# Packing the state-space parameters and the first input on the host, a shifted tap load, Y in column strips, and new planner costs

## The chip, the cores and the metric

The kernel runs on one core of a Trainium2 chip. The time is device time in microseconds, one launch of the whole program; lower is better. The core has TensorE (PE), VectorE (DVE), ScalarE (ACT), GpSimd (POOL) and SyncE (SP), which here issues all DMA loads and stores of the program. Every engine takes its own instructions strictly in the order of its queue.

## The reference

A sequence of 256 tokens of width 1024 goes through two blocks in float32. The first has four layers; each is a mixer (differential attention, stick-breaking attention, sliding-window attention with a sink, differential attention again) and a SwiGLU feed-forward, with an RMS norm before and after each. The second block has dilated attention on one half of the width and, on the other half (512 channels in 32 groups of 16), a diagonal complex state-space model (S5) of 64 states per group, and then a gated projection of an extra input p. Cut to the state-space part, which the change concerns most:

```python
dt = exp(log_dt)[:, None]
a = exp(lam_re * dt) * (cos(lam_im * dt) + i sin(lam_im * dt))
bb = (a - 1) / lam * (b_re + i b_im)
bu = einsum('bsgc,gnc->bsgn', u, bb)
x[s] = a * x[s-1] + bu[s]
y = einsum('bsgn,gcn->bsgc', x_re, c_re) - einsum('bsgn,gcn->bsgc', x_im, c_im) + d_skip * u
yg = gelu(y)
out = yg * sigmoid(yg @ w_glu + b_glu)
```

The rest of the work is mostly dense products of the 256 tokens with weights.

## The kernel before, in words

**Dense products.** Tokens are in two halves b of 128 (NB = 2). To reach float32 accuracy each operand is split into a high and a low part (fp32r), and each product runs three passes. A weight chunk of 1 MB (128 x 2048 elements) is loaded into one of three buffers `raw`; ScalarE makes the high part and VectorE the low part (`w`, 11 buffers, two splits for a chunk on each engine); on TensorE the activations are stationary, and 512 columns of the weights move per pass into a PSUM tile `acc`. The activations are `hnT` (normed input, transposed), `hT` (hidden of the feed-forward) and `oT` (attention output). `prenorm` (L717) turns x with TensorE transposes `tr`, multiplies by the transposed gains gT and splits.

**State space.** Time is cut into 32 blocks k of 8 steps t. `ssm_prep_tasks` (L1196) computes, during the first layers, what depends on the parameters alone: `params` (L1214) loads them with 39 DMAs into `pp` and `pt` and clears the taps, `coef` (L1255) forms the discretised coefficients on GpSimd, ScalarE and VectorE and turns C with TensorE (`cT`), `powers` (L1303) the powers of a (tiles `q`), and `part_e`, eight times (L1322), wide GpSimd products of 128 x 256, which TensorE transposes (`eT`) and multiplies (`ke`) into the taps, the response within 15 steps. `part_g` (L1356) makes G, which leads from states to outputs. E, G and taps are stored in DRAM (`scrE`, `scrG`, `taps`). These tasks are spread over the first layers' steps.

In the second block `ssm_in` (L1387) makes U, the inputs of each block of time; `ssm_scan` (L1406) forms S = E U with 64 small matmuls, copies it from PSUM to X, and VectorE and GpSimd run the scan over the 32 blocks; `ssm_y` (L1455) adds taps times U and G times X in two PSUM tiles Y: 32 tap products with 128-column taps stationary (loaded in two rounds of eight DMAs) and 32 moving columns, and 32 products with G stationary (loaded in four rounds of four DMAs), on a copy X2 of X that has the real part over the imaginary one. Y is copied out, written to DRAM (`scr_y`), read back transposed, and goes through the Gelu. Dense products of attention's q, k, v and gates are recorded around these steps.

**What sets the order.** The code only records the engine calls (`record`, L209). `_Program` gives each a cost in nanoseconds (`passes` L170 for TensorE, `cost` L185 for the others and for DMAs), with edges for data and for buffers that are used again (`ring_edges` L261) and for the first loads in a list by hand (`head_edges` L284). `schedule` (L426) then runs a list scheduler forward and backward from several random starts, keeps the order whose modelled end is the earliest, and `issue` (L456) issues that order; all instructions have line L464 in the profile. So a changed cost or a dropped operation can move any instruction on any engine. The costs of a dense pass and of a GpSimd operation before are

```python
load, stream, k = cols / 1.2, n * (1.0 if n >= 256 else 4.0) / 2.4, 1
return 150 + (1.66 if op == ALU.mult else 2.1) * n
```

**Start.** `setup` (L544) loads the gains and x, turns the gains with one transpose, starts the first weights, and sets the order of the first loads in `nc.head`; `warm` (L572) runs eight matmuls while they come.

## Time and profile before

| what | us |
|---|---|
| runs of the kernel before, three | 1449.31, 1451.95, 1452.11 |
| median | 1451.95 |
| span of the profiled execution | 1446.5 |
| its own time, beside the span | not listed apart; the runs shown lie 2.8 to 5.6 over the span |
| TensorE busy | 1399.7 |
| VectorE, ScalarE, GpSimd busy | 900.2, 774.7, 163.4 |

The profile is of one execution, and its times count from the start of its span. A busy TensorE is not necessarily one at its peak: the clock that it was granted (PEclk, 1.00 is full) is listed by stretch. The views used are the page's table of busy times, its table of DMA issues, the chain of waits (start, length, engine and tile, number of instructions), the timeline of an engine (start, length, engine, line, operation, tile written and tiles read, shape, count, and in brackets the idle time before it with what ended it), and the table of stretches.

### The profile page before, as it was taken

Reading aid. Unit: us, or ns where it says so; the run is one execution under the profiler, and the core shown is the slowest. Engines: PE = TensorE matmul, PEld = TensorE weight load, DVE = VectorE, ACT = ScalarE, POOL = GpSimd, SP = SyncE. Lnnn points to the kernel's source line nnn. Section 1 sums busy time; section 2 is a strip of 40 time slices with the busy share of each in tenths; the row PEclk is TensorE's granted clock in tenths of the full one; section 3 lists DMA queues with packets and bytes.
Section 4 is the critical chain, followed back from the end, with each engine's and each line's share of the span. In section 5 each row is a group of like instructions: output and inputs, shape, how many; then the busy total and the mean of one; then the engine's idle time right before and its main releaser. Section 6 shows DMA issues by size and latency. Waiting matters only on the chain.

```text
span 1446.5 us, 18484 instructions
## 1 busy us (share of the span) xinstructions
PE 1399.7 (97%) x7093; PEld 1157.0 (80%) x7093; DVE 900.2 (62%) x1311; ACT 774.7 (54%) x1261; POOL 163.4 (11%) x258
## 2 busy tenths in 40 slices
PE   8999969699999999999999999999999999998998
PEld 6788847578788788888878888887888888887887
DVE  7967526556855755557856456588766555676274
ACT  6656525334776754445656454456665444562572
POOL 0001039961200000000000000010010000010000
PEclk9999989899999999999999999999999999997999
DMA  8644527554634455555334555554445555467641
GB/s 265 204 146 153 182 27 258 164 191 160 212 116 146 143 192 178 197 178 180 128 116 141 194 180 196 182 187 147 151 154 204 175 190 185 156 218 149 197 147 54
DMA packets 153360, 243.95 MB, mean 169 GB/s; under 512 B 23016, under 2 KB 45880, under 8 KB 153272
## 3 DMA queue, kind: packets, MB, share of 16 engines
q1 hardware_dynamic: 153272, 242.77, 51.7%
q8 instruction: 56, 0.92, 0.3%
q14 instruction: 32, 0.26, 0.1%
HBM read 235.97 MB, written 6.78 MB: 168 GB/s over the span
## 4 chain that ended last, share of the span: by engine, by line
PE 86%; POOL 6%; SPq 3%; DVE 2%; DMA 2%; issue 1%; ACT 1%; DVEq 0%; POOLq 0%
PE acc L464 73%; POOL pt L464 4%; PE tr L464 4%; SPq L464 3%; PE sS L464 2%; PE sc L464 2%; PE Y L464 1%; PE z L464 1%; PE oS L464 1%; DMA scrM<-taps 1%; POOL pp L464 1%; PE o L464 1%; DVE w L464 1%; POOL q L464 1%; PE asT L464 0%
## 5 line engine op out<-in xcount | busy, mean ns | idle before, releaser
L464 PE MATMUL acc<-w,hnT 128*128 128x512 f32 (+1 forms) x3744 | 849.7, 381 | 3.0 <-ACT hnT L464 1.0
L464 PEld LDWEIGHTS acc<-w,hnT 128*128 128x128 f32 x3744 | 664.2, 190 | 133.4 <-issue 4.8
L464 DVE TENSOR_TENSOR w<-raw,w 128x1024 fp32r<-128x1024 f32 (+1 forms) x431 | 519.3, 1220 | 195.6 <-ACT w L464 185.9
L464 ACT ACTIVATE w<-raw 128x1024 fp32r<-128x1024 f32 (+1 forms) x431 | 442.1, 1041 | 194.2 <-PE acc L464 151.8
L464 PE MATMUL acc<-w,hT 128*128 128x512 f32 x1056 | 256.6, 398 | 13.2 <-ACT hT L464 13.0
L464 PEld LDWEIGHTS acc<-w,hT 128*128 128x128 f32 x1056 | 198.6, 191 | 54.9 <-ACT hT L464 13.4
L464 PE MATMUL acc<-w,oT 128*128 128x512 f32 x480 | 119.2, 397 | 0.0
L464 PEld LDWEIGHTS acc<-w,oT 128*128 128x128 f32 x480 | 87.9, 188 | 19.8 <-issue 2.3
L464 POOL TENSOR_TENSOR po_r<-po_v,neghalf 128x1 f32<-128x1 f32 x16 | 13.8, 862 | 751.5 <-DVE po_v L464 751.4
L464 ACT ACTIVATE sg<-acc,pn_r 128x512 f32<-128x512 f32 (+1 forms) x48 | 31.2, 650 | 81.2 <-PE acc L464 77.3
L464 DVE SCALAR_TENSOR_TENSOR sg<-acc,pn_r,sg 128x512 f32<-128x512 f32 (+1 forms) x48 | 33.8, 704 | 50.2 <-PE acc L464 40.4
L464 ACT ACTIVATE hT<-tr 128x512 fp32r<-128x512 f32 (+1 forms) x48 | 26.7, 556 | 71.1 <-PE tr L464 71.0
L464 POOL TENSOR_TENSOR pt<-pp 128x256 f32<-128x256 f32 x64 | 50.6, 808 | 42.9 <-PE ke L464 41.0
L464 DVE TENSOR_TENSOR hT<-tr,hT 128x512 fp32r<-128x512 f32 (+1 forms) x48 | 30.9, 644 | 30.6 <-ACT hT L464 30.5
L464 DVE TENSOR_TENSOR facc<-acc,facc 128x512 f32<-128x512 f32 x32 | 21.9, 687 | 33.7 <-PE acc L464 33.7
L464 POOL TENSOR_TENSOR pn_r<-pn_v,neghalf 128x1 f32<-128x1 f32 x20 | 16.2, 810 | 213.0 <-DVE pn_v L464 201.0
L464 ACT ACTIVATE ad_e<-sc,ad_nm 128x128 f32<-128x128 f32 (+1 forms) x64 | 26.1, 422 | 24.2 <-DVE ad_nm L464 20.6
L464 ACT ACTIVATE hnT<-gx 128x512 fp32r<-128x512 f32 x40 | 25.1, 627 | 20.0 <-DVE gx L464 19.9
L464 POOL TENSOR_TENSOR pt<-pt 128x256 f32<-128x256 f32 x32 | 35.5, 1108 | 2.0
L464 ACT ACTIVATE sqj<-x 128x512 f32<-128x512 f32 x40 | 24.9, 625 | 18.6 <-DVE x L464 13.8
L464 DVE TENSOR_REDUCE as_nm<-sS 128x2 f32<-128x512 f32 (+2 forms) x20 | 12.5, 635 | 35.7 <-PE sS L464 35.7
L464 DVE TENSOR_TENSOR hnT<-gx,hnT 128x512 fp32r<-128x512 f32 x40 | 27.8, 696 | 5.4 <-ACT hnT L464 4.7
(225 smaller groups left out, 1113.5 us busy)
## 6 DMA issues: line engine op xcount, KB each, us to landing
raw<-in_ffn_w_gate_dram SPq DMA_DIRECT2D x44, 1024.0 KB, 5.2
raw<-in_ffn_w_up_dram SPq DMA_DIRECT2D x44, 1024.0 KB, 5.2
raw<-in_ffn_w_down_dram SPq DMA_DIRECT2D x32, 1024.0 KB, 5.2
raw<-in_a_w_in_dram SPq DMA_DIRECT2D x22, 1024.0 KB, 5.2
raw<-in_ffn_w_down_dram SPq DMA_DIRECT2D x16, 768.0 KB, 4.5
raw<-in_b_w_in_dram SPq DMA_DIRECT2D x12, 1024.0 KB, 5.2
raw<-in_w_in_dram SPq DMA_DIRECT2D x12, 1024.0 KB, 5.3
raw<-in_a_w_out_dram SPq DMA_DIRECT2D x8, 1024.0 KB, 5.1
```

The lines of the kernel that those rows point to most:

```text
L464: r = getattr(getattr(self.nc, op.eng), op.call)(*op.args, **op.kw)
```

## The change

It has four parts. (1) The planner's costs: a gap is added to each pass (a dense pass of 512 columns now counts 226.5 ns instead of 215), narrow float32 matmuls are divided by the number of column strips, DMA costs depend on the length of contiguous runs, and GpSimd costs are higher. (2) The host lays out four arrays: the gains transposed (gT), the input x transposed (xT), p transposed (pT), and all state-space parameters in one array of 128 x 1584 (ssm). The transposes of x ahead of layer 0, of the gains, of C and of p are dropped, and `params` has two loads. (3) The taps are stored as 240 rows of 512, and one load for each half reads them with overlapping rows. S is computed for blocks 0 to 30 and written shifted by one. (4) In Y, U and X are stationary (32 columns, one column strip for each quarter j of the groups) and taps and G move (128 columns); G takes 64 products of 64 rows instead of 32 of 128. Y is copied to SBUF and turned by eight transposes, and the Gelu reads PSUM; the trip through DRAM is dropped.

```diff
 def passes(method, args):
         if method == "transpose":
-            return 53.0, 53.5, 2
+            return 53.0, 52.0, 2, 2.0
         lhsT, rhs = args[1], args[2]
         cols, n = _size(lhsT), _size(rhs)
         if rhs.dtype == F32:
-            load, stream, k = cols / 1.2, n / 1.2, 2
+            tiles = 128 // max(32, min(cols, 128))
+            load, stream, k, gap = cols / 1.2, n / 1.2 / tiles, 2, 5.3 / tiles
         elif rhs.dtype == F32R:
-            load, stream, k = cols / 1.2, n * (1.0 if n >= 256 else 4.0) / 2.4, 1
+            load, stream, k, gap = cols / 1.2, n * (1.0 if n >= 256 else 4.0) / 2.4, 1, 13.2
...
+    def dma_cost(out, src):
+        dram = src if src.space == DRAM else out
+        run = 1
+        for step, count in reversed(list(dram.ap)):
+            if step != run:
+                break
+            run *= count
+        total = out.shape[0] * _size(out)
+        spread = 16.0 / min(16, out.shape[0], src.shape[0])
+        return max(total * 4 / 360.0, total / min(run, 2048) * 4.0) * spread
...
         if method == "dma_start":
-            return out.shape[0] * _size(out) * 4 / 360.0
+            return _Program.dma_cost(out, kw["in_"])
...
         if op == ALU.pow:
-            return 300 + 164.5 * n
-        return 150 + (1.66 if op == ALU.mult else 2.1) * n
+            return 690 + 120 * n
+        return 150 + (2.1 if op == ALU.mult else 2.7) * n
...
 def setup(self):
+        nc.sync.dma_start(out=self.gT, in_=a["gT"])
+        self.xT0 = []
+        for b in range(NB):
+            self.xT0.append([self.t2a(b, "xT0") for _ in range(2)])
+        for h in range(2):
+            nc.sync.dma_start(out=self.xT0[0][h], in_=a["xT"][:, h * 512:(h + 1) * 512])
...
-        nc.head = [loads[i] for i in (1, 4, 5, 0, 2, 6, 3, 7, 8, 11, 9)]
+        nc.head = [loads[i] for i in (3, 1, 0, 2, 4)] + loads[5:]
...
 def prenorm(self, b, g):
+            if g == 0:
+                tp = gx = self.xT0[b][h].rearrange("p (j q) -> p j q", j=4)
+            else:
+                tp = self.xpose(b, x[:, h * 512:(h + 1) * 512], 4)
+                gx = self.t2a(b, "gx").rearrange("p (j q) -> p j q", j=4)
...
 def params():
-            for src, dst in (("lambda_re_2", lre), ("lambda_im_2", lim)):
-                nc.sync.dma_start(out=dst, in_=a[src][0].rearrange("(g h) n -> (h n) g", h=2))
-            for h in range(2):
-                nc.sync.dma_start(
-                    out=ldt[64 * h:64 * h + 64, :],
-                    in_=a["log_dt_2"][0].rearrange("(g h) -> h g", h=2)[h].partition_broadcast(64))
...
+            nc.sync.dma_start(out=st["pp"][:, :1072], in_=a["ssm"][:, :1072])
+            nc.sync.dma_start(out=t[:, 1024:1536], in_=a["ssm"][:, 1072:])
...
 def coef():
-            tp = self.sc("cT").rearrange("p (j q) -> p j q", j=4)
-            for j in range(4):
-                nc.tensor.transpose(tp[:, j, :], st["cn"][:, j // 2, j % 2].rearrange("p h n -> p (h n)"), self.ident)
...
 def part_e(q):
-                for t in range(8):
-                    nc.sync.dma_start(out=self.taps[:, :, 7 + t, :], in_=st["ke"][16 * t:16 * t + 16])
+                nc.sync.dma_start(out=self.taps[112:, :], in_=st["ke"].rearrange("p g c -> p (g c)"))
...
 def ssm_scan(self, st):
-                        nc.tensor.matmul(sp[r][64 * h:64 * h + 64, gp, :], E[:, g, r, 64 * h:64 * h + 64],
-                                         U[:, self.gidx(2 * gp + h), :], start=(gp == 0), stop=(gp == 15))
+                        nc.tensor.matmul(sp[r][64 * h:64 * h + 64, gp, 1:], E[:, g, r, 64 * h:64 * h + 64],
+                                         U[:, self.gidx(2 * gp + h), :31], start=(gp == 0), stop=(gp == 15))
...
+        nc.gpsimd.memset(X3[:, :, :, 0], 0.0)
...
 def ssm_y(self, st):
-                nc.tensor.matmul(yp[g % 2][:, g // 2, :], m[:, gg, :], U[:, self.gidx(g), :], start=(g < 2), stop=False)
...
-                    nc.tensor.matmul(yp[h][:, gp, 1:32], G[:, g, h, :], X2[:, gp, h, 0:31], start=False, stop=(gp == 15))
...
+            nc.sync.dma_start(out=m, in_=bass.AP(taps.tensor, taps.offset + 256 * q, [[512, P], [16 * 512, 8], [1, 256]]))
...
+                    nc.tensor.matmul(yp[g8 % 2][32 * j:32 * j + 32, g8 // 2], U[:, self.gidx(g), :], ms[q][:, :, x:x + 16],
+                                     start=(g8 < 2), stop=False)
+        for j in range(4):
+            G = self.scr_tile("scrG", 1024)
+            nc.sync.dma_start(out=G, in_=self.scr["G", j])
...
+                        nc.tensor.matmul(yp[h][32 * j:32 * j + 32, g], X3[pr, r, 4 * j + g, :], G[pr, g, r],
+                                         start=False, stop=(g == 3 and r == 1))
...
+                nc.tensor.transpose(tp[:, t, :], Y[:, 4 * u + t].rearrange("p g h f -> p (g h f)"), self.ident)
...
 def proj_fn(ch, j):
-                    for bb in range(NB):
-                        pt = self.t2a(bb, "pTin")[:, :256]
-                        nc.sync.dma_start(out=pt, in_=a["p_2"][0, 0, bb * P:(bb + 1) * P, :])
-                        self.xpose_split(bb, pt, st["pT"], 2 * bb, n=2)
+                    pt = self.t2a(0, "pTin")
+                    nc.sync.dma_start(out=pt, in_=a["pT"])
...
+def _layouts(i):
+    rows = np.concatenate([i["norm_gains"][:, ::2].reshape(-1, KT, P), i["mix_norm_2"].reshape(-1, KT, P),
+                           i["ple_norm_2"].reshape(-1, KT, P)])
...
+    cols = [lam(i["lambda_re_2"][0]), lam(i["lambda_im_2"][0]), lam(dt)]
+    cols += [mat(i[k][0].transpose(0, 2, 1)) for k in ("c_re_2", "c_im_2")]
+    cols.append(np.broadcast_to(i["d_skip_2"][0], (P, 512)))
+    cols += [mat(i[k][0]) for k in ("b_re_2", "b_im_2")]
+    return {
+        "gT": rows.transpose(2, 0, 1).reshape(P, 80),
+        "xT": i["x"][0].reshape(NB, P, KT, P).transpose(3, 0, 2, 1).reshape(P, -1),
+        "pT": i["p_2"][0, 0].reshape(NB, P, 2, P).transpose(3, 0, 2, 1).reshape(P, -1),
+        "ssm": np.concatenate(cols, axis=1),
+    }
```

The order of the instructions on an engine follows from the planner. In the rows below a count is of calls; a float32 matmul call is two passes in the trace, a dense call one.

**SyncE's queue at the loads of the parameters** (raw is a weight chunk; pp and pt hold parameters). Before:

```order
L464 DMA raw<-in_ffn_w_gate_dram 128x4x512 x2
L464 DMA pp<-in_lambda_re_dram 128x16x1
L464 DMA pp<-in_log_dt_dram 64x16x1 x2
L464 DMA pp<-in_lambda_im_dram 128x16x1
L464 DMA pt<-in_b_re_dram 128x16x16
L464 DMA pt<-in_b_im_dram 128x16x16
L464 DMA pt<-in_c_re_dram 16x2x64 x16
L464 DMA pt<-in_c_im_dram 16x2x64 x16
L464 DMA taps<-pt 512x1x112
L464 DMA raw<-in_ffn_w_up_dram 128x4x512 x2
L464 DMA raw<-in_ffn_w_gate_dram 128x4x512
```

After:

```order
L478 DMA raw<-in_ffn_w_gate_dram 128x4x512 x2
L478 DMA pp<-in_ssm_dram 128x1072
L478 DMA pt<-in_ssm_dram 128x512
L478 DMA taps<-pt 112x512
L478 DMA raw<-in_ffn_w_up_dram 128x4x512 x2
L478 DMA raw<-in_ffn_w_gate_dram 128x4x512 x2
```

Both stand behind the same two gate loads. The 38 parameter loads have become two, and the load of d_skip, which stood further back, is in the first of them.

**TensorE around the first two parts of E** (eT transposes a part of E, ke multiplies it; acc is a dense product). Before:

```order
L464 MATMUL acc<-w,hnT 128x512 x24
L464 MATMUL cT<-ident,pt 128x128 x4
L464 MATMUL acc<-w,hT 128x512 x24
L464 MATMUL acc<-w,hnT 128x512 x24
L464 MATMUL eT<-ident,pt 128x128 x4
L464 MATMUL ke<-pt 128x32 x3
L464 MATMUL acc<-w,hnT 128x512 x9
L464 MATMUL ke<-pt 128x32
L464 MATMUL acc<-w,hnT 128x512 x15
L464 MATMUL tr<-ident,sg 128x128 x4
L464 MATMUL acc<-w,hnT 128x512 x48
L464 MATMUL eT<-ident,pt 128x128 x4
```

After:

```order
L478 MATMUL acc<-w,hT 128x512 x24
L478 MATMUL acc<-w,hnT 128x512 x48
L478 MATMUL tr<-ident,sg 128x128 x4
L478 MATMUL acc<-w,hnT 128x512 x24
L478 MATMUL eT<-ident,pt 128x128 x4
L478 MATMUL ke<-pt 128x32 x2
L478 MATMUL acc<-w,hnT 128x512 x19
L478 MATMUL ke<-pt 128x32 x2
L478 MATMUL acc<-w,hnT 128x512 x9
L478 MATMUL eT<-ident,pt 128x128
L478 MATMUL acc<-w,hnT 128x512 x11
L478 MATMUL eT<-ident,pt 128x128 x3
```

The transposes of C are gone. The second eT, which had 72 dense matmuls between it and the first, now comes after 28. The rows of GpSimd that lead to it in the changed kernel end with the powers q and then the wide products:

```order
L478 TENSOR_TENSOR q_419<-q_419,pp 128x16
L478 TENSOR_TENSOR pp<-q_419 128x16
L478 TENSOR_TENSOR q_419<-q_419,pp 128x16
L478 TENSOR_TENSOR pt<-pp 128x256
L478 TENSOR_TENSOR pt<-pt 128x256
L478 TENSOR_TENSOR pt<-pp 128x256 x2
L478 TENSOR_TENSOR pt<-pt 128x256
L478 TENSOR_TENSOR pt<-pp 128x256
L478 TENSOR_TENSOR pt<-pt 128x2x128
```

Before, the powers stood among the wide products of the first part; now they stand in front of the second. Between the first eT's last operand and the second's there are 42 operations of 16 columns and 10 wide ones.

**TensorE between the last S and Y** (S_..., Y_... are PSUM tiles of the two halves, tr and acc dense work). Before:

```order
L464 MATMUL S_1926<-ssm,scrE 64x32 x8
L464 MATMUL acc<-w,hnT 128x512 x8
L464 MATMUL tr<-ident,qk2sb 128x128 x4
L464 MATMUL acc<-w,hnT 128x512 x18
L464 MATMUL tr<-ident,qk2sb 128x128 x4
L464 MATMUL acc<-w,hnT 128x512 x8
L464 MATMUL Y_1948<-ssm,scrM 128x32 x8
L464 MATMUL Y_1949<-ssm,scrM 128x32 x2
L464 MATMUL acc<-w,hnT 128x512 x2
L464 MATMUL Y_1949<-ssm,scrM 128x32 x2
L464 MATMUL acc<-w,hnT 128x512 x2
L464 MATMUL Y_1949<-ssm,scrM 128x32
```

After:

```order
L478 MATMUL S_1918<-ssm,scrE 64x31 x2
L478 MATMUL tr<-ident,qk2sb 128x128 x4
L478 MATMUL acc<-w,hnT 128x512 x41
L478 MATMUL Y_1939<-scrM,ssm 32x128 x8
L478 MATMUL Y_1940<-scrM,ssm 32x128 x8
L478 MATMUL acc<-w,hnT 128x512 x36
L478 MATMUL Y_1939<-scrM,ssm 32x128 x8
L478 MATMUL Y_1939<-scrG,ssm 32x128
L478 MATMUL Y_1940<-scrM,ssm 32x128 x8
L478 MATMUL Y_1940<-scrG,ssm 32x128 x8
L478 MATMUL Y_1939<-scrG,ssm 32x128 x15
L478 MATMUL tr<-ident,qk2sb 128x128 x4
```

Before, 34 dense matmuls and eight transposes lie between the last S and the first tap product, and then dense matmuls in small numbers among the products. Now 41 lie ahead of the taps and 36 ahead of G, whose products come in runs of eight on one strip; only nine lie among them.

## Rows read from the trace of the kernel before

**Rows 1.** The page's first part: busy time, share of span, instructions.

```profile
PE 1399.7 (97%) x7093; PEld 1157.0 (80%) x7093; DVE 900.2 (62%) x1311; ACT 774.7 (54%) x1261; POOL 163.4 (11%) x258
```

**Rows 2.** The chain of waits: start, length, engine, tile, passes.

```profile
126.30 15.01 PE acc L464 x66
...
435.82 1.08 PE z L464 x8
...
453.50 1.90 PE oB L464 x32
...
1269.98 0.44 PE tr L464 x4
```

**Rows 3.** Stretches: length; PE, PEld, DVE, ACT, POOL busy; clock; DMA share; GB/s.

```profile
190.40:203.40 13.00, 0.02 (x1) 0.02 (x1) 5.08 (x16) 5.25 (x8) 0.73 (x4) 0.70 0.42 28
203.40:207.30 3.90, 3.71 (x8) 2.51 (x9) 2.69 (x7) 1.65 (x3) 3.74 (x16) 0.50 0.09 17
264.40:268.80 4.40, 4.01 (x17) 3.45 (x17) 2.04 (x4) 1.07 (x2) 4.16 (x7) 0.50 0.02 4
270.00:300.00 30.00, 27.36 (x134) 22.77 (x133) 18.27 (x21) 11.35 (x13) 28.98 (x34) 0.96 0.60 193
296.00:303.00 7.00, 5.33 (x22) 4.80 (x22) 1.82 (x4) 1.19 (x2) 6.69 (x11) 0.65 0.54 193
1306.50:1356.20 49.70, 44.48 (x220) 39.28 (x219) 22.43 (x57) 10.97 (x15) 0.99 (x1) 0.76 0.63 145
1320.60:1340.50 19.90, 19.85 (x79) 18.53 (x80) 9.37 (x24) 2.54 (x3) 0.00 (x0) 0.50 0.33 66
1356.20:1440.00 83.80, 83.80 (x424) 69.28 (x424) 51.83 (x83) 52.24 (x72) 1.97 (x2) 1.00 0.42 137
```

**Rows 4.** Timelines of SyncE, TensorE and ScalarE, 168 to 204 us.

```profile
168.67 3.09 SPq L464 DMA_DIRECT2D raw<-in_ffn_w_gate_dram  x2
...
178.05 16.42 SPq L464 DMA_DIRECT2D pp<-in_lambda_im_dram  x1
...
170.56 5.74 PE L464 MATMUL acc<-w,hT 128*128 128x512 f32 x24
...
203.38 1.22 PE L464 MATMUL acc<-w,hT 128*128 128x512 f32 x2 [13.01 <-ACT hT L464]
...
194.68 0.22 ACT L464 ACTIVATE pp<-pp 128x16 f32<-128x16 f32 x1 [14.62 <-DMA pp<-in_log_dt_dram]
```

**Rows 5.** Timelines of GpSimd and TensorE, 195 to 265 us.

```profile
195.73 0.39 POOL L464 TENSOR_TENSOR pp<-pp 128x16 f32<-128x16 f32 x2 [50.46 <-DMA pp<-in_lambda_re_dram]
...
250.95 1.20 POOL L464 TENSOR_TENSOR q<-q 128x16 f32<-128x16 f32 x1
...
255.54 0.22 POOL L464 TENSOR_TENSOR q<-q 128x16 f32<-128x16 f32 x1
...
228.52 0.60 PE L464 MATMUL eT<-ident,pt 128*128 128x128 f32 x4
...
264.38 0.47 PE L464 MATMUL eT<-ident,pt 128*128 128x128 f32 x1 [10.59 <-POOL pt L464]
```

**Rows 6.** Timeline of TensorE at the first tap product.

```profile
1320.65 4.45 PE L464 MATMUL Y<-ssm,scrM 128*128 128x32 f32 x20 [5.22 <-DMA scrM<-taps]
```

**Rows 7.** The page's DMA issues: count, KB each, us to landing.

```profile
g<-in_norm_gains_dram SPq DMA_DIRECT2D x8, 512.0 KB, 4.8
```

**Rows 8.** Stretches, GpSimd alone: length, busy (count), clock, DMA share, GB/s.

```profile
264.40:313.72 49.32, 47.52 (x56) 0.87 0.53 169
```

**Rows 9.** Stretches, TensorE's scores of attention (sS) alone, same columns.

```profile
1306.50:1356.20 49.70, 1.44 (x6) 0.76 0.63 145
```

**Rows 10.** Timeline of VectorE: first and last operation of the scan.

```profile
1307.24 0.40 DVE L464 TENSOR_TENSOR scA<-ssm,q 128x128 f32<-128x128 f32 x1 [1.47 <-ACT ssm L464]
...
1329.03 0.51 DVE L464 TENSOR_TENSOR ssm<-ssm,scA 128x336 f32<-128x336 f32 x1
```

**Rows 11.** Timeline of TensorE: the first dense matmuls.

```profile
10.47 4.19 PE L464 MATMUL acc<-w,hnT 128*128 128x512 f32 x9
```

More of the change, by code (lines that the diff above doesn't have):

```diff
@@ L351, in forward @@
             elif e == "tensor":
-                load, stream, k = op.passes
+                load, stream, k, gap = op.passes
                 group = op.group
@@ L563, in setup @@
             self.prep(1)
+        for h in range(2):
+            nc.sync.dma_start(out=self.xT0[1][h], in_=a["xT"][:, 1024 + h * 512:1536 + h * 512])
+        nc.sync.dma_start(out=self.x[0], in_=xsrc[:P, :])
+        self.ident = cp.tile([P, P], F32, name="ident")
+        nc.sync.dma_start(out=self.ident, in_=self.consts_dram[:, COFF["ident"][0]:COFF["ident"][0] + P])
+        nc.sync.dma_start(out=self.x[1], in_=xsrc[P:, :])
         loads = [o for o in nc.ops if o.eng == "sync"]
-        nc.sync.dma_start(out=self.x[1], in_=xsrc[P:, :])
-        loads.append(nc.ops[-1])
-        nc.head = [loads[i] for i in (1, 4, 5, 0, 2, 6, 3, 7, 8, 11, 9)]
+        nc.head = [loads[i] for i in (3, 1, 0, 2, 4)] + loads[5:]
         self.neghalf = cp.tile([P, 8], F32, name="neghalf")
@@ L1468, in ssm_y @@
-        for q in range(2):
-            m = self.scr_tile("scrM", 2048).rearrange("p (g x) -> p g x", g=16)
-            for t in range(8):
-                nc.sync.dma_start(out=m[16 * t:16 * t + 16],
-                                  in_=self.taps[:, 16 * q:16 * q + 16, t:t + 8, :].rearrange("c g t f -> c g (t f)"))
-            for gg in range(16):
-                g = 16 * q + gg
-                nc.tensor.matmul(yp[g % 2][:, g // 2, :], m[:, gg, :], U[:, self.gidx(g), :], start=(g < 2), stop=False)
@@ L1494, in ssm_y @@
-        st["ygT"] = st["X"].rearrange("p (b j k t) -> p b j k t", b=NB, j=4, k=16)
-        for b in range(NB):
-            nc.scalar.activation(st["ygT"][:, b], yT.rearrange("p t (j k) -> p j k t", j=4)[:, :, b * 16:(b + 1) * 16, :],
-                                 AF.Gelu)
+        yp = [self.sc(f"Y{h}").rearrange("p (g t f) -> p g t f", g=4, t=8) for h in range(2)]
+        taps = self.taps[:, :]
+        ms = []
+        for q in range(2):
+            m = self.scr_tile("scrM", 2048).rearrange("p (t x) -> p t x", t=8)
+            nc.sync.dma_start(out=m, in_=bass.AP(taps.tensor, taps.offset + 256 * q, [[512, P], [16 * 512, 8], [1, 256]]))
+            ms.append(m)
@@ new lines, in ssm_y @@
+        for q in range(2):
+            for g8 in range(8):
+                for j in range(2 * q, 2 * q + 2):
+                    g = 8 * j + g8
+                    x = 16 * (g % 16)
+                    nc.tensor.matmul(yp[g8 % 2][32 * j:32 * j + 32, g8 // 2], U[:, self.gidx(g), :], ms[q][:, :, x:x + 16],
[3 more added lines that the diff above has]
+            nc.sync.dma_start(out=G, in_=self.scr["G", j])
+            G = G.rearrange("p (g r t f) -> p g r t f", g=4, r=2, t=8)
+            for g in range(4):
+                for r in range(2):
+                    for h in range(2):
+                        pr = slice(64 * h, 64 * h + 64)
+                        nc.tensor.matmul(yp[h][32 * j:32 * j + 32, g], X3[pr, r, 4 * j + g, :], G[pr, g, r],
+                                         start=False, stop=(g == 3 and r == 1))
@@ L1706 @@
     arrays, aps = {}, {}
-    for name in NAMES:
-        arr = np.ascontiguousarray(inputs[name])
+    given = {name: inputs[name] for name in NAMES} | _layouts(inputs)
+    for name, arr in given.items():
+        arr = np.ascontiguousarray(arr)
         key = f"in_{name}_dram"
```

94 lines of the change are left out of this document (28 added, 66 removed).

## The prediction

> **What bounds the kernel now.** I read the page's first part first. TensorE is busy 97% of a span of 1446.5 us, all other engines far less [rows 1]. So the kernel is bound by the columns that TensorE streams, except where it stands still or is granted half its clock. The chain of waits gives the price of its main work: 66 dense matmuls of 512 columns in 15.01 us, 227 ns each [rows 2]. The table of stretches then shows where that rate is lost: around 190 to 303 us and 1306 to 1356 us TensorE stands still, and for a while after it stood the granted clock is 0.50, which is 1.2 of 2.4 GHz [rows 3]. Next came the timelines of the two places.
>
> At the first, SyncE spends 16.42 us on issuing one load, lambda_im, which brings four bytes per element. ScalarE, strictly in order, sits 14.62 us in front of an exponential that needs the log_dt load issued just ahead of it; behind that exponential stands the copy of hT, and TensorE waits 13.01 us for it [rows 4]. About 60 us later it waits 10.59 us more for a part of E that GpSimd has not finished [rows 5]. At the second place it waits 5.22 us for taps [rows 6], then does 19.85 us of work at clock 0.50 [rows 3].
>
> All times below are reckoned against the profiled execution. The page gives its span alone; the median of the runs, 1451.95, is 5.5 us over the span, and I add that at the end.
>
> **Prep of the state space.** Removed: the loads of lambda, log_dt, B and d_skip, 32 loads of C, and four transposes of C. Added: two loads of 536 and 256 KB from one packed array. What was lost here and has its cause in these loads or in GpSimd's lateness: 13.0 us of standing [rows 4], 10.6 us [rows 5], and 30.00 - 27.36 = 2.6 us between 270 and 300 us [rows 3], so 26.2 us. Work done at half the clock costs half its time: 3.71/2 + 4.01/2 + 5.33 x 0.35 = 5.8 us [rows 3]. Together 32.0 us.
>
> What comes back? The packed load stands behind the same two gate loads, issued from 168.67 to 171.76; TensorE began its first hT matmul at 170.56, my zero for this part [rows 4]. Half a MB in size, like the gain whose landing takes 4.8 us [rows 7], and behind 2 MB in flight, it lands at 6 to 9; I take 8. Before, GpSimd's first product (195.73) and the first eT (228.52), which did not wait, are 32.8 us apart [rows 5]; in the new order GpSimd has a product of 512 columns and eight small ones more in front, but no late lambda_im and no late taps, so I leave 31.5. The first part of E is ready at 39.5. In the new order TensorE reaches the first eT after 216 dense matmuls and eight transposes (0.44 us for four, [rows 2]), 49.0 + 0.9 = 49.9: no wait, 10.4 us in hand. From there it has 28 matmuls and four small products, 7.3 us, before the second eT, while GpSimd has 10 wide operations and 42 of 16 columns. A small one took 0.22 us when alone and 1.20 us at worst [rows 5]; the operations around the wide ones ran at 47.52/56 = 0.85 us each, or 0.88 with the gaps [rows 8]. That is 10 x 0.88 + 42 x 0.22 = 18.0 us, or 21.8 us with a tenth of the small ones slow. Less 7.3 and 10.4, TensorE waits 0.3 to 4.1 us. The five later parts need 12 operations each, 10.6 us, and TensorE comes for them after some 44 dense matmuls, 10.1 us: up to 2.5 us more. I take 4 us, near the middle of 0 to 7, and 2 us for the clock behind it. So 26.0 us are gained here, between 21 and 32.
>
> GpSimd's slow 1.20 us would fit a rule of the Trainium skill (GPSIMD Engine Reference, section Specifications): its SBUF interfaces are shared with VectorE, and it contends with VectorE instructions that have two SBUF inputs. By it every weight split on VectorE could slow GpSimd.
>
> **The Y product and what follows.** The marks are the last S matmul and the last Y matmul. Before, that stretch is 49.70 us [rows 3]. In it the order has 75 dense matmuls and eight transposes (17.0 + 0.9 us), and 1.4 us of scores [rows 9]; 30.4 us are left for Y, its wait and the half clock. Now Y is 96 products of two passes each. The 32 tap products alternate between two column strips; the nearest row is oB, which alternates two halves: 1.90 us for 32 passes, 59 ns each [rows 2], so 64 x 0.059 = 3.8 us. The 64 G products come in runs of eight on one and the same strip. A run on one tile is shown by z: eight passes occupy 1.08 us, 135 ns each [rows 2]. The lower end for 128 passes is 59 ns again (7.6 us), the upper 135 ns (17.3 us); I take 115 ns, 14.7 us, nearer to z, since the runs are of its kind.
>
> Does G wait for the scan? VectorE's scan began at 1307.24, 0.7 us after the last S, and ended at 1329.54 [rows 10]: 22.3 us, of which about 3.3 us were other operations and 1.1 us is half a weight split at its end. In the new order four splits (4.6 us) stand within it: 0.7 + 22.3 - 4.4 + 4.6 = 23.2 us. TensorE's own work ahead of the first G is 77 dense matmuls, four transposes and 48 tap passes: 17.5 + 0.4 + 2.8 = 20.7 us. So it waits 2.5 us. The two tap loads and four G loads replace 32 small ones; they share the three raw buffers with the last weight chunk, the second tap load gets its buffer only after two splits in the scan, and they come about as late as X, so they add nothing to that wait. Y now costs 3.8 + 14.7 + 2.5 = 21.0 us, 9.4 less, with bounds from the two prices of G and 3 us of half clock.
>
> Eight transposes of Y cost 0.9 us; the four of p are gone (0.4), and so is a wait of about 0.9 us within S, since 12 of the dense matmuls now lie among its passes. The round trip of Y through DRAM ran beside dense work, for TensorE is busy 83.80 of 83.80 us after it [rows 3], so its loss is worth nothing by itself. In all 9.8 us, between 4 and 19.
>
> The Trainium skill (TensorEngine Tiling (Array Packing), section Theoretical Speedup) promises up to four times for 32 columns; by it the 192 passes would cost a quarter of their 135 ns, an estimated 6.5 us. Its section Key Properties also speaks against the change: changing the tiling mode drains TensorE. No run here isolates that.
>
> **Start.** No transposes of x in front of layer 0 (16, and one of the gains), and the first dense matmul, which began at 10.47 [rows 11], no longer waits for x to be turned. With the weights' first slice now issued first I expect it about 4 us earlier. But three more weight loads stand ahead of the second half of x, 1 MB of xT is added, and the splits of the second chunk stand behind the norm of both halves, which needs the last x. So most of that is lost again: +3 us, between -2 and +6.
>
> **Everything else.** The planner now takes 226.5 instead of 215 ns for a dense matmul. The old error left other engines slack; without it some waits of a microsecond can come up in attention: -2 us, between -10 and 0. The transposes of C and of the gains that are gone: +0.6.
>
> **Sum.** 26.0 + 9.8 + 3.0 - 2.0 + 0.6 = 37.4 us; 1446.5 - 37.4 + 5.5 = 1414.6, so **1415 us**.
>
> **Rivals.**
> - Strips run abreast. If two strips always overlapped twice as well as oB's halves, 192 passes at 29.5 ns would cost 5.7 instead of 18.5 us; with nothing lost at the eT (6 us), 1415 - 12.8 - 6 = 1396. For it speaks that oB's alternating passes take less than half of z's; against it that the runs of G stay on one strip. Chance 0.17.
> - The clock falls in Y. The 2.5 us wait and 20 us of narrow passes resemble what stood ahead of 1320.60 [rows 3]. Some 14 us of work at half the clock cost 7 us, and with G at its upper end (2.6) and another wait of 4 us at the second eT: 1429. Against it: in the new order dense work lies right ahead of the taps and between them and G. Chance 0.25.
> - The loads do not help. If the packed load lands so late that the exponential blocks ScalarE again for 13 us, with the half clock behind it, half of the prep's gain is gone: 1415 + 16 = 1431. Chance 0.05.
> - Slower: GpSimd decides. If splits on VectorE hold GpSimd at 1.7 us per wide operation throughout, a part takes 20.4 us against TensorE's 10.1, and six waits of 10.3 us make 62 us in place of the 4 taken: 1473. The point from which it makes the kernel slower is (37 + 4)/6 + 10.1 = 16.9 us a part, or 1.4 us an operation. Against it stands 0.88, measured with the splits running [rows 8]. Chance 0.05.
>
> **Numbers.** The forecast as summed, 1402 to 1424, has 0.46, and 0.02 are left for no change. A measurement of this kernel tells about 0.2% from no change. Faster by more: 0.46 + 0.17 + 0.25 + 0.05 = 0.93; same 0.02; slower 0.05. The range of 1395 to 1434 leaves out the last rival, no change, and the far ends of the first two.
>
> **What would show it.** No wait of ScalarE for pp over 4 us, none of TensorE for hT; SyncE's load of pp issued in about a microsecond; a wait of 0 to 7 us for GpSimd at the second eT; G passes near 115 ns; the clock at 0.50 only briefly after 200 us. Wrong would be: GpSimd over 1.4 us per wide operation, a half clock that outlasts Y, or TensorE idle in the attention layers.

## The result, and the profile after

The changed kernel takes 1417.74 us (median of four runs, 1415.19 to 1417.83), the one before on the same chip 1451.23: the ratio is 0.977, with a 95% interval of 0.9756 to 0.9784. Forecast were 1415 us and a range of 1395 to 1434. The profiled span is 1415.5 us, 31.0 less than before. The run that was profiled lies only 2.2 us over that span, where 5.5 had been added, so the forecast's own span, 1409.1, was 6.4 us too low.

The page's first part, after (the row that answers to [rows 1]):

```profile
PE 1390.8 (98%) x7140; PEld 1145.2 (81%) x7140; DVE 899.2 (64%) x1307; ACT 771.7 (55%) x1258; POOL 168.1 (12%) x259
```

TensorE's busy time fell by 8.9 us, its idle time from 46.8 to 24.7. To see where, I count dense matmuls (all with output acc, 5328 in each kernel, in nearly the same order) in TensorE's timeline and take the start of the 480th (layer 0's feed-forward), the 2100th (past the prep of the state space) and the 4870th (before S) as marks. So the table gives stages of equal dense work, in us, from one profiled execution of each kernel:

| kernel | start, to 480 | prep, to 2100 | middle, to 4870 | S, Y and end | span |
|---|---|---|---|---|---|
| before | 153.2 | 456.0 | 669.7 | 167.6 | 1446.5 |
| after | 158.4 | 429.5 | 669.3 | 158.3 | 1415.5 |
| difference | +5.2 | -26.5 | -0.4 | -9.3 | -31.0 |
| forecast | -3.0 | -26.0 | +1.4 | -9.8 | -37.4 |

(The forecast's "everything else" and the few transposes stand in the middle column.) Three stages came as forecast; the start did not. Now the rows of each.

**Prep.** Timelines of SyncE, GpSimd and TensorE, after (they answer to [rows 4] and [rows 5]):

```profile
177.10 0.46 SPq L478 DMA_DIRECT2D pp<-in_ssm_dram  x1
...
183.33 0.22 POOL L478 TENSOR_TENSOR pp<-pp 128x16 f32<-128x16 f32 x1 [33.68 <-DMA pp<-in_ssm_dram]
...
226.92 0.60 PE L478 MATMUL eT<-ident,pt 128*128 128x128 f32 x4
...
239.52 0.47 PE L478 MATMUL eT<-ident,pt 128*128 128x128 f32 x1 [4.70 <-POOL pt L478]
...
274.41 0.33 PE L478 MATMUL eT<-ident,pt 128*128 128x128 f32 x1 [0.89 <-POOL pt L478]
...
286.56 0.33 PE L478 MATMUL eT<-ident,pt 128*128 128x128 f32 x1 [1.05 <-POOL pt L478]
...
288.56 1.38 PE L478 MATMUL ke<-pt 128*128 128x32 f32 x6 [1.53 <-POOL pt L478]
```

The load is issued in 0.46 us instead of 16.42, and lands, with its first hT matmul at 175.81 as zero, at 7.5 us. No wait for hT is left. The first eT comes at 51.1 us (49.9 forecast) and does not wait; the second waits 4.70 us, and the four waits for GpSimd sum to 8.2. ScalarE waits for pp at most 1.1 us at a time.

**The clock and the Y stage.** Stretches, after (columns as in [rows 3]): the two half-clock stretches of the prep, the stretch from the last S to the last Y, and the end:

```profile
237.50:244.30 6.80, 4.78 (x12) 3.82 (x13) 6.74 (x10) 0.00 (x0) 6.49 (x7) 0.50 0.48 154
288.70:295.50 6.80, 6.80 (x21) 5.63 (x22) 1.29 (x3) 1.29 (x2) 6.56 (x11) 0.50 0.24 87
1288.20:1326.00 37.80, 37.63 (x291) 31.35 (x287) 21.21 (x52) 8.99 (x11) 0.00 (x0) 1.00 0.53 173
1326.00:1409.60 83.60, 82.55 (x417) 67.35 (x417) 52.09 (x82) 50.28 (x73) 2.77 (x2) 1.00 0.36 122
```

Timeline of TensorE in Y, after (it answers to [rows 6]):

```profile
1298.12 1.94 PE L478 MATMUL Y<-scrM,ssm 128*32 128x128 f32 x32
...
1311.27 4.17 PE L478 MATMUL Y<-scrG,ssm 64*32 64x128 f32 x44 [0.17 <-DVE ssm L478]
...
1320.09 5.95 PE L478 MATMUL Y<-scrG,ssm 64*32 64x128 f32 x64
...
1382.93 0.50 PE L478 MATMUL acc<-w,pT 128*128 128x512 f32 x1 [1.05 <-ACT pT L478]
```

49.70 us between the last S and the last Y became 37.80, with eleven dense matmuls more in it, and the clock stays at 1.00. To the start of the next instruction the 32 tap passes take 1.87 us, 58 ns each; the last 64 G passes, in runs on one strip, 5.88 us, 92 ns each. G waits 0.17 us for the scan. Between the last S and the last Y the idle time fell by 5.1 us, and what the dense matmuls took over 227 ns each by 5.6.

Summed over TensorE's timeline from each instruction's start to the next, Y's passes alone went from 19.1 to 16.5 us. That is no gain of the strips. Before, the 64 tap passes ran at half the clock and took 12.8 us, while G's 64 passes, already at full clock, took 6.3 us, some 100 ns each:

```profile
1347.57 1.20 PE L464 MATMUL Y<-X,scrG 128*128 128x31 f32 x10
```

After, G's 128 passes take 12.6 us at the same clock, twice as much. At full clock the old Y would have taken about 12.7 us, an estimate (half of 12.8, and 6.3). So the strips as written here add some 3.7 us of work, and what Y gained is its wait and its clock.

**Start.** Timelines of SyncE, ScalarE and TensorE, after:

```profile
2.59 8.61 SPq L478 DMA_DIRECT2D raw<-in_a_w_in_dram  x4
10.82 0.37 SPq L478 DMA_DIRECT2D raw<-in_a_w_in_dram  x1
...
11.24 0.94 SPq L478 DMA_DIRECT2D xT<-in_xT_dram  x2
12.22 0.43 SPq L478 DMA_DIRECT2D x<-in_x_dram  x1
...
18.46 0.63 ACT L478 ACTIVATE sqj<-x 128x512 f32<-128x512 f32 x1 [0.62 <-DMA x<-in_x_dram]
...
25.01 1.99 ACT L478 ACTIVATE w<-raw 128x1024 fp32r<-128x1024 f32 x2
...
7.14 1.22 PE L478 MATMUL acc<-w,hnT 128*128 128x512 f32 x2 [2.53 <-ACT hnT L478]
10.10 2.54 PE L478 MATMUL acc<-w,hnT 128*128 128x512 f32 x5 [1.74 <-DVE hnT L478]
...
26.10 0.73 PE L478 MATMUL acc<-w,hnT 128*128 128x512 f32 x2 [1.34 <-ACT w L478]
28.33 2.12 PE L478 MATMUL acc<-w,hnT 128*128 128x512 f32 x6 [1.50 <-DVE w L478]
```

The first dense matmul is 3.3 us earlier than in [rows 11]. But SyncE spends 8.61 us on four weight loads. The first two go out at once; the other two need buffers, and the last, in a row of its own above, goes out at 10.82. The second half of xT and x are issued only after it. TensorE's idle time in this stage rose from 5.4 to 9.2 us. So ScalarE takes the first squares of x at 18.46 and splits the second chunk only at 25.01. Before, the same two rows of ScalarE are

```profile
5.52 0.63 ACT L464 ACTIVATE sqj<-x 128x512 f32<-128x512 f32 x1 [3.50 <-DMA x<-in_x_dram]
...
20.71 2.01 ACT L464 ACTIVATE w<-raw 128x1024 fp32r<-128x1024 f32 x2 [0.77 <-DMA raw<-in_a_w_in_dram]
```

### The profile page after: what moved, and what is told of

Same layout as the page of the kernel before. It is cut to its first block, busy times and chain, and to the rows that moved or that the text cites. A ratio compares the mean times of both kernels' runs of the same rounds, so it can differ in the third digit from the quotient of the medians.

```text
span 1415.5 us, 18447 instructions
## 1 busy us (share of the span) xinstructions
PE 1390.8 (98%) x7140; PEld 1145.2 (81%) x7140; DVE 899.2 (64%) x1307; ACT 771.7 (55%) x1258; POOL 168.1 (12%) x259
## 4 chain that ended last, share of the span: by engine, by line
PE 87%; POOL 5%; DVE 4%; DMA 2%; ACT 1%; issue 1%; SPq 0%; DVEq 0%; ACTq 0%; POOLq 0%
PE acc L478 74%; PE tr L478 3%; POOL pt L478 3%; POOL pp L478 2%; PE sS L478 2%; PE sc L478 2%; PE z L478 1%; PE oS L478 1%; DVE w L478 1%; PE Y L478 1%; DMA raw<-in_w_ple_gate_dram 1%; PE o L478 1%; DVE scA L478 1%; PE asT L478 1%; POOL q L478 1%
## 5 line engine op out<-in xcount | busy, mean ns | idle before, releaser
L478 PE MATMUL acc<-w,hT 128*128 128x512 f32 x1056 | 251.7, 393 | 0.0
L478 POOL TENSOR_TENSOR po_r<-po_v,neghalf 128x1 f32<-128x1 f32 x16 | 12.7, 795 | 778.2 <-DVE po_v L478 778.2
L478 ACT ACTIVATE sg<-acc,pn_r 128x512 f32<-128x512 f32 (+1 forms) x48 | 31.2, 651 | 80.6 <-PE acc L478 80.5
L478 POOL TENSOR_TENSOR pt<-pp 128x256 f32<-128x256 f32 x64 | 55.4, 883 | 2.4 <-PE ke L478 1.6
L478 ACT ACTIVATE hnT<-gx 128x512 fp32r<-128x512 f32 x36 | 22.7, 629 | 22.9 <-DVE gx L478 22.8
L478 ACT ACTIVATE ad_e<-sc,ad_nm 128x128 f32<-128x128 f32 (+1 forms) x64 | 26.2, 422 | 15.2 <-DVE ad_nm L478 14.8
L478 DVE TENSOR_TENSOR hnT<-gx,hnT 128x512 fp32r<-128x512 f32 x36 | 24.7, 687 | 6.5 <-ACT hnT L478 5.8
L478 PE MATMUL tr<-ident,sg 128*128 128x128 f32 x176 | 27.3, 274 | 0.9 <-DVE sg L478 0.9
```

The lines of the kernel that those rows point to most:

```text
L478: r = getattr(getattr(self.nc, op.eng), op.call)(*op.args, **op.kw)
```

## The experiments

All were run in pairs with the kernel before. Each changed line can move the whole order, since the planner's search starts anew; therefore the stages are compared, by the marks above, as differences to the kernel before. The median and the ratio are of all runs of a kernel, the stages and the span of its profiled run alone:

| kernel | median | ratio (95%) | start | prep | middle | end | span |
|---|---|---|---|---|---|---|---|
| b_prep | 1439.45 | 0.9917 (0.9901 to 0.9934) | +0.8 | -18.0 | +3.2 | +3.4 | 1435.9 |
| b_lam | 1439.35 | 0.9906 (0.9877 to 0.9935) | +1.0 | -17.3 | +0.7 | +0.3 | 1431.2 |
| b_taps | 1443.03 | 0.9933 (0.9918 to 0.9948) | +0.9 | +6.2 | -4.0 | -7.3 | 1442.3 |
| b_y | 1443.88 | 0.9961 (0.9935 to 0.9987) | +0.8 | -0.7 | +1.0 | -6.8 | 1440.8 |
| a_oldcost | 1422.32 | 0.9811 (0.9778 to 0.9843) | +2.9 | -26.7 | +2.6 | +2.5 | 1427.8 |
| a_oldpool | 1419.80 | 0.9786 (0.9759 to 0.9812) | +4.3 | -22.2 | +2.3 | -13.1 | 1417.8 |
| a_nostart | 1410.62 | 0.9721 (0.9700 to 0.9743) | 0.0 | -29.1 | +0.3 | -9.7 | 1408.0 |
| a_head | 1425.49 | 0.9814 (0.9780 to 0.9849) | +1.3 | -27.0 | +5.6 | -2.8 | 1423.6 |
| a_alt | 1404.00 | 0.9665 (0.9652 to 0.9678) | +3.1 | -31.2 | -1.6 | -14.8 | 1402.0 |
| a_pad | 1430.93 | 0.9850 (0.9836 to 0.9863) | +4.7 | -26.2 | -0.7 | +5.6 | 1429.9 |
| ns_alt | 1409.88 | 0.9700 (0.9683 to 0.9716) | -0.4 | -29.4 | +1.8 | -10.9 | 1407.6 |
| ns_alt_s7 | 1403.16 | 0.9657 (0.9644 to 0.9671) | -0.2 | -30.9 | +1.0 | -15.2 | 1401.2 |

The profiled run of b_lam was 6.4 us quicker than its median and that of a_oldcost 7.2 us slower; the others lie within 2 us. How far a stage moves without any edit there shows in a_pad: its start, prep and middle have the order of the changed kernel and differ from it by 0.5, 0.3 and 0.3 us.

### b_prep: the packed parameters alone

```diff
 (the kernel before)
-  39 loads of lambda, log_dt, B, C, d_skip; four transposes of C
+            nc.sync.dma_start(out=st["pp"][:, :1072], in_=a["ssm"][:, :1072])
+            nc.sync.dma_start(out=t[:, 1024:1536], in_=a["ssm"][:, 1072:])
```

> The kernel before, with the state-space parameters packed by the host and read in two loads, and nothing else of the change (old planner costs, old taps, old Y, old start). If the packed load alone carries the gain of the prep stage (no 16 us issue, ScalarE not blocked, GpSimd some 20 us earlier), the span falls by 22 to 28 us, to 1418 to 1425, and no wait of TensorE for GpSimd over 5 us is left. If the new costs of GpSimd in the planner are needed to place the transposes of E, only the wait of 13.0 us and its half clock go: span 1430 to 1433, with a wait near 10 us for GpSimd still there.

Measured: 18.0 us in the prep stage, and neither case: the block of ScalarE is gone, but waits for GpSimd remain, in two steps at the third eT:

```profile
241.57 0.48 PE L464 MATMUL eT<-ident,pt 128*128 128x128 f32 x1 [5.29 <-POOL pt L464]
243.57 0.90 PE L464 MATMUL eT<-ident,pt 128*128 128x128 f32 x3 [1.53 <-POOL pt L464]
```

Counted to the 660th dense matmul the gain is 16.4 us, the same to 0.1 us as in the changed kernel, b_lam, a_oldcost, a_oldpool and a_alt: the block of ScalarE with its half clock. After that mark b_prep gains 1.6 us more, the changed kernel 10.1. From there to the 2100th TensorE stands still for 17.0 us in the kernel before, 16.0 in b_prep and 9.0 in the changed kernel, and the half clock takes 6.4, 8.1 and 5.8 us. Elsewhere 7.4 us are lost again, 3.4 of them at the end, where the late taps are still there.

### b_lam: lambda and log_dt alone

```diff
 (the kernel before)
-  the loads of lambda_re, lambda_im and log_dt
+            nc.sync.dma_start(out=st["pp"][:, :48], in_=a["ssm"][:, :48])
```

> The kernel before, with lambda_re, lambda_im and log_dt alone read from the packed array in one load; B, C in 32 loads and d_skip stay. If the issue of lambda_im is what blocked ScalarE, its 14.6 us wait is gone here too and at least 15 us are gained: span 1420 to 1432, the lower end if GpSimd's earlier start also removes the wait of 10.6 us. If the long row of small C loads behind it would have blocked the queue anyway, weight loads come late and TensorE waits for splits instead: less than 10 us gained.

Measured: 17.3 us in the prep stage, within a microsecond of packing everything, and the medians of the two agree to 0.1 us. The 48 columns carry the whole fixed gain; the 32 loads of C, still issued one by one, cost nothing that shows. The span of 1431.2 is that of its quickest run; the four lie between 1432.98 and 1442.78, so by the median it falls short of the forecast. Waits for GpSimd of 4.00 us and less remain, and one of 4.65 us for VectorE (tile sg):

```profile
246.20 0.33 PE L464 MATMUL eT<-ident,pt 128*128 128x128 f32 x1 [4.00 <-POOL pt L464]
```

### a_oldcost and a_oldpool: the change without the planner's new costs

```diff
 (the changed kernel, a_oldcost)
-  the gap in passes, the strips, dma_cost, GpSimd's costs
+  the costs of the kernel before
 (the changed kernel, a_oldpool)
-            return 690 + 120 * n
-        return 150 + (2.1 if op == ALU.mult else 2.7) * n
+            return 300 + 164.5 * n
+        return 150 + (1.66 if op == ALU.mult else 2.1) * n
```

> The changed kernel with the planner's old costs for TensorE, DMAs and GpSimd; all loads and products as changed. If the costs are what gave the other 9 us in the prep stage (the packed load alone gave 17 of 26) and the other 3 to 4 in Y (Y alone gave 6 of 9.5), this is 10 to 14 us slower than the changed kernel: span 1425 to 1430, with waits of 10 us or more for GpSimd at the transposes of E. If those differences came from how the parts of the change act together, it stays within 4 us of the changed kernel, 1413 to 1420.

> The changed kernel with the old costs of GpSimd alone (1.66 and 2.1 ns per element instead of 2.1 and 2.7, and the old power); TensorE's gap and the DMA costs as changed. If the prep stage needs GpSimd's cost to place the transposes of E, the waits for GpSimd there are 10 to 20 us in place of 8.2 and the span is 1420 to 1428. If the gap of TensorE's passes does it, the span is 1413 to 1419.

Measured: with all old costs the prep stage gains 26.7 us, as with the new ones, so the costs are not what the prep needs: that theory falls. With GpSimd's old costs alone it gains 22.2. After the 660th matmul the gain is 10.3, 5.8, 10.1 (the changed kernel), 14.8 (a_alt) and 1.0 to 1.6 (b_lam, b_prep) us: a spread by the order that the planner happened on, with no cost that explains it. In b_lam and b_prep TensorE still stands 16.0 us there, nearly as long as before; what in their orders makes it wait was not settled.

The end is another matter: in its profiled run a_oldcost loses 11.8 us there against the changed kernel, and TensorE is at half clock for 23.9 us in Y:

```profile
1308.70:1332.60 23.90, 23.84 (x137) 0.50 0.38 133
```

(Stretch, length, TensorE busy, clock, DMA share, GB/s.) Three waits of 1.8 to 1.9 us lie in Y from 1295 us on. The other three runs took 1420.77 to 1423.06, 6 to 9 us less, at a mean granted clock of 0.990 to 0.994 against 0.986. So the clock need not have fallen like this in all of them; by the medians the whole kernel loses 4.6 us against the changed one.

### b_taps: the late taps taken away

```diff
 (the kernel before)
-            for t in range(8):
-                nc.sync.dma_start(out=m[16 * t:16 * t + 16], ...)
+            nc.sync.dma_start(out=m.rearrange("p g x -> p (g x)"), in_=self.a["w_in_2"][0][P * q:P * q + P, :2048])
```

> The kernel before, but the tap products read 1 MB of weights, fetched by one plain load, in place of the taps fetched by eight loads for each half (so the state-space output is not the reference's); the form of the products, G and the trip of Y through DRAM stay. If the late taps cause both the wait of 5.2 us and the half clock behind it, both go: 9 to 14 us gained, span 1433 to 1438, clock 1.00 in Y. If the narrow products of Y themselves pull the clock down, only the wait goes: 4 to 6 us gained, and a stretch at 0.50 stays in Y.

Measured: between both cases. The wait of 5.2 us is gone and the end gains 7.3 us, but the clock still falls, for 13.6 us (TensorE alone, columns as just above). The nearest wait ahead, of 0.68 us, ended 13.6 us earlier:

```profile
1324.30:1337.90 13.60, 13.60 (x52) 0.50 0.16 46
```

So the clock can fall among the old Y passes, 32 columns each between pairs of dense matmuls, without a wait. In the kernel before, with the wait, it was down for 23.8 us (1318.7 to 1342.5). Two of the four runs of b_taps were 2 and 5 us shorter at a mean clock of 0.986 against 0.980, so it need not fall each time. The +6.2 us in the prep stage are another order there.

### b_y: the Y part alone

```diff
 (the kernel before)
+  taps in [240, 512] and one shifted load per half, S shifted, Y in strips, eight transposes
-  eight loads per half, X2, scr_y
```

> The kernel before, with the taps read in one shifted load, S shifted, Y in column strips with transposes in place of the trip through DRAM, and nothing else (old planner costs, old prep, old start). If the Y part's gain does not depend on the other parts, 8 to 11 us are gained, span 1436 to 1438, with a clock of 1.00 in Y and G passes near 92 ns. If the old costs place the products badly (they count a narrow pass four times too long), TensorE waits for the scan or the clock falls: 0 to 5 us gained.

Measured: 6.8 us at the end, between both cases. The passes of G take 5.5 us for 60, 92 ns, as forecast; but taps and G wait 1.67, 2.83 and 0.63 us. Three of its ten runs took 1453 to 1457 us, as long as the kernel before; what slowed them no trace shows. TensorE's timeline:

```profile
1321.13 1.94 PE L464 MATMUL Y<-scrM,ssm 128*32 128x128 f32 x38 [1.67 <-DMA scrM<-taps]
...
1329.53 0.41 PE L464 MATMUL Y<-scrG,ssm 64*32 64x128 f32 x4 [2.83 <-issue]
```

### a_nostart and a_head: the start

```diff
 (the changed kernel, a_nostart)
-  gT and xT from the host
+  setup and prenorm of the kernel before
 (the changed kernel, a_head)
-        nc.head = [loads[i] for i in (3, 1, 0, 2, 4)] + loads[5:]
+        nc.head = [loads[i] for i in (3, 1, 0, 2, 4, 5, 10, 8, 9, 12, 6, 11, 7)]
```

> The changed kernel with the start of the kernel before: x and the gains turned on TensorE, the first loads in the old order. The changed kernel is 5.2 us later than the one before when layer 0's attention begins and stays so. If the new start costs this, the span falls by 4 to 6 us, to 1410 to 1412. If the planner's costs in layer 0 cause it, the span stays at 1414 to 1417.

> The changed kernel with xT and gT kept, but the list of first loads in another order: both halves of x and the second half of xT ahead of the last two weight loads of the first chunk, which wait for a buffer. If the start is lost because x and xT stand behind those blocked loads, the span falls by 3 to 6 us, to 1409 to 1413. If the added 1 MB of xT is what costs (the DMA engines are full in the first 27 us), 0 to 2 us are gained.

Measured: with the old start the stage takes 153.2 us, as before, and the whole kernel 1410.62 us, 7 less than the changed one. So the new start costs 5.2 us here, and with the old start the new costs lose nothing. The loss is not the same in every order: with the same first loads it is 2.9 us in a_oldcost, 3.1 in a_alt, 4.3 in a_oldpool and 4.7 in a_pad. With xT kept and the loads in another order (a_head) 1.3 us are left. So the order of the first loads makes most of the loss, 1.6 to 3.9 us of it, and about 1.3 us remain for the rest, the added megabyte with it. The total of a_head is nevertheless worse, for the clock fell in Y, behind a wait of 1.19 us, and G's passes took 142 ns:

```profile
1313.18 13.08 PE L478 MATMUL Y<-scrG,ssm 64*32 64x128 f32 x92 [1.19 <-DVE ssm L478]
```

### a_alt: G's products in two strips in turn

```diff
 (the changed kernel)
-        for j in range(4):
+        for jj in range(2):
+            (loads of G for j = 2 * jj and 2 * jj + 1)
...
                     for h in range(2):
+                        for j in (2 * jj, 2 * jj + 1):
```

> The changed kernel with the G products written so that successive ones of a Y tile go to two column strips in turn (two G loads ahead of each pair of strips), as the tap products do; nothing else. If a run on one strip is what holds G at 92 ns per pass while taps in two strips take 58, G falls to about 60 ns: 128 passes save 4 us, span 1410 to 1413. If G's pace is set by its 64 rows or its loads, it stays at 85 to 95 ns and the span at 1414 to 1417; a wait for the second pair's loads would add to that.

Measured: faster than expected, 1404.00 us. Timeline of TensorE:

```profile
1304.86 3.07 PE L478 MATMUL Y<-scrG,ssm 64*32 64x128 f32 x64 [0.26 <-DVE ssm L478]
...
1312.40 3.27 PE L478 MATMUL Y<-scrG,ssm 64*32 64x128 f32 x60
```

To the start of the next instruction that is 47 to 53 ns per pass in place of 92. The starts of single passes in the traces show how: in the changed kernel most follow 109 ns after one another, within a product and from one product to the next, and some closer; in a_alt two start 6 or 7 ns apart, and the next two about 110 ns after them. So one strip starts a pass every 109 ns here, and two strips run side by side. The end is 5.5 us shorter than in the changed kernel, which the passes explain (124 x 0.04 = 5.0). The other 8 us of the span come from the start (2.1), the prep (4.7) and the middle (1.2), where nothing was edited: another order.

### a_pad: the scan 3 us longer

```diff
 (the changed kernel, in issue)
+                for _ in range(10 if op.pad is not None else 0):
+                    self.nc.vector.tensor_tensor(op.pad, op.pad, op.pad, op=ALU.max)
```

> The changed kernel with ten more operations of 128 columns on VectorE in the scan, put in behind the planner's back, so that every other instruction keeps its place: X is about 3 us later. TensorE waited 0.17 us for X; now it waits about 3 us in the middle of the narrow products, the wait that the prediction expected. If such a wait there pulls the clock down (the rival that priced it at 7 us), the span grows by 8 to 12 us, to 1423 to 1428, with a stretch at 0.50. If the clock holds, only the wait is paid: 1418 to 1419.

Measured: every instruction stands where it stood, TensorE waits 2.42 us in place of 0.17, and the kernel takes 1430.93 us, 13 more than the changed one and more than either case. Timelines of VectorE and TensorE, and TensorE's stretch (columns as above):

```profile
1305.50 3.23 DVE L480 TENSOR_TENSOR scA<-scA 128x128 f32<-128x128 f32 x10
...
1310.71 0.51 DVE L481 TENSOR_TENSOR ssm<-ssm,scA 128x336 f32<-128x336 f32 x1
...
1311.32 0.60 PE L481 MATMUL Y<-scrG,ssm 64*32 64x128 f32 x2 [2.42 <-issue]
...
1313.70 8.33 PE L481 MATMUL Y<-scrG,ssm 64*32 64x128 f32 x46
...
1311.30:1331.70 20.40, 20.38 (x98) 0.50 0.32 104
```

The profile names no releaser for the wait ("issue"), but it ends 0.1 us after the scan writes the real part of X. The 46 passes of G after it take 180 ns each, twice their 92. Of the 14.9 us lost at the end, 2.3 are the wait, 1.4 a longer wait for pT, and the rest, some 11 us, is work at half clock. This is the rival "the clock falls in Y", made on purpose. It had priced the half clock at 7 us; that its total, 1429, is near the measured one is chance.

### ns_alt and ns_alt_s7: a version of both

```diff
 (ns_alt: the changed kernel with the edits of a_nostart and a_alt; ns_alt_s7 besides)
-    tries, seed = 24, 346
+    tries, seed = 24, 7
```

> The changed kernel with the start of the kernel before and with G's products alternating between two strips. If both gains add up, the span is 1403 to 1405, the fastest of all. If the clock falls in Y (a new order of the planner with a wait of 1 us or more in front of G), some 7 us are lost again: 1410 to 1412.

> The same computation as the version with the old start and alternating G, but the planner's random numbers start elsewhere (7 in place of 346), which gives another order of the same instructions, with two or three dense matmuls between the small groups of S. If that version lost its gain only because the clock fell at a wait of 1 us within S, this one runs S and Y at full clock and has a span of 1397 to 1402, below the 1402.0 of the version with alternating G alone. If other orders lose as much somewhere else (a wait for GpSimd, the clock in S or Y), it is 1404 to 1412.

Measured: ns_alt 1409.88, since the clock fell within S, from 1278.7 to 1288.9, 1.5 us after a wait of 0.99 us between narrow passes (timeline of TensorE, and its stretch):

```profile
1277.18 0.42 PE L478 MATMUL S<-ssm,scrE 128*64 128x31 f32 x8 [0.99 <-DMA scrE<-scrE]
...
1278.70:1288.90 10.20, 10.20 (x62) 0.50 0.54 183
```

With other random numbers the same instructions take 1403.16 us, the fastest of all, with S and Y at full clock. It is not clearly faster than a_alt (1404.00): a wait of 4.1 us for GpSimd came up in the prep.

## Why the prediction was right, and where not

- **Prep, 26.0 us: measured 26.5.** The fixed part is settled: 16.4 us, from the 48 columns of lambda and log_dt alone. The load landed at 7.5 us (8 taken). TensorE's idle time was to fall by 22.2 us net, 26.2 less 4, and between the marks fell by 21.1, from 30.2 to 9.0. The waits for GpSimd were 8.2 us, over the 7 that bounded them. Its wide products took 0.88 to 1.03 us each in the mean (0.88 taken), so the rival in which GpSimd decides did not come. Other losses went that had not been counted, among them waits of 1.35 us around 222 us and 1.7 us around 370. The half clock was mis-sized on both sides, since its stretches were cut too short. It costs half of TensorE's busy time in them: 9.3 us before, by the rows below (TensorE alone), where the prediction had 5.8 (its terms add up to 5.7), and 5.8 after, where it had 2. The difference, 3.5 us, is near the 3.8 taken. So the mechanism held, but that the sum came out is partly luck, and the spread by the order (1 to 15 us for the same GpSimd work) was not in the argument.

```profile
195.70:209.30 13.60, 5.73 (x13) 0.50 0.33 33
257.10:270.80 13.70, 6.04 (x24) 0.50 0.27 105
298.10:304.90 6.80, 6.80 (x25) 0.50 0.32 122
```

- **Y, 9.8 us: measured 9.3.** Taps: 3.8 taken, 3.9 measured. G: 14.7 taken at 115 ns, 12.6 measured, 92 ns in the long runs. Its wait: 2.5 taken, 0.17 measured. So Y was 4.4 us cheaper than forecast; some three of these were given back, by narrow S passes that now alternate with single dense ones (about 2 us) and the new wait for pT (1.05). The forecast put the half clock down to the wait for taps; b_taps shows that it can fall among the old passes without it.
- **The wait that did not come.** X was complete 23.0 us after the last S, as forecast (23.2). But sixteen more tap passes, and four of G that need only the real part of X, which is done earlier, lay ahead of the products that need all of it. TensorE's work up to there took 22.9 us instead of 20.7. The forecast's main case had TensorE wait 2.5 us at full clock. a_pad has such a wait, and takes 13 us more. That the wait fell away was luck, and it kept the time near 1415.
- **Strips.** The lower bound of 59 ns, from oB, was about right for passes that alternate and z's 135 too high for those that do not. The Trainium skill (TensorEngine Tiling (Array Packing), section Key Properties) states that different tiles can work in parallel; a_alt agrees: in turn on two strips 47 to 53 ns, on one 92. The estimate of 6.5 us for the 192 passes by the same page was not reached: they took 16.5 us in the changed kernel and 10.4 in a_alt.
- **Start, +3 us: measured -5.2, outside the -2 to +6 that was given.** This is the step that failed. "Most of that is lost again" was right in kind, but of 4 us only 1 was taken off, and the loss was 8.5: from 3.3 us ahead at the first dense matmul to 5.2 behind. SyncE's queue stands in order, and two loads that wait for one of three buffers held up the second half of xT until 11.24 and x until 12.22.
- **Everything else, -2.0 us: 0.4 us gained in the middle stage.** The new costs did no harm there that shows.
- **Around the span.** The gains were forecast 6.4 us too large, which the start alone (8.2) explains; the 5.5 us added around the span, of which 2.2 were there, hid 3.3 of it. The 5.5 was the median less the profiled span. Where a run lists both its time and its span, they are 1.8 to 2.2 us apart, so the profiled execution of the kernel before was probably some 3 us quicker than the median, and the differences of spans come out that much too small: 31.0 us, where the medians differ by 33.5.

## What to carry to other kernels

Look for what is queued behind a slow load: 48 columns brought in one piece gave 16 us here, packing the rest gave nothing that could be shown. In a stretch of narrow matmuls a wait of 1 to 3 us can cost several times its length through the clock, so keep dense work around it and leave slack for the operand that comes last. Put successive products on different column strips: in runs on one strip they cost more here than the full-width form that they replaced. And where a planner draws the order, run several of its orders, each several times, before a gain of a few microseconds is ascribed to an edit.

## What the runs showed that I had not expected

A wait of 2.42 us in Y cost 14.9 us at the end, by a granted clock of 0.50 over 20.4 us. Yet in ns_alt_s7 a wait of 1.17 us at the same place left the clock at 1.00 (first row: TensorE's timeline; second: its stretch), while 1.19 us in a_head brought it down; in the first G alternates and its passes are half as long, which may be the difference, but was not tried by itself. Nor does one order always behave alike: three runs of a_head took 1425.39 to 1428.04 us at a mean clock of 0.986 to 0.988, the fourth 1417.99 at 0.992. And orders of the same instructions differ by 6.7 us in the total (ns_alt against ns_alt_s7).

```profile
1304.81 2.85 PE L478 MATMUL Y<-scrG,ssm 64*32 64x128 f32 x60 [1.17 <-DVE ssm L478]
...
1300.00:1322.00 22.00, 20.83 (x196) 1.00 0.51 184
```
